# Four more gathered rows in the space of the transposed input, with an earlier first use and an earlier fetch of the residual

## The chip, the cores and the metric

The kernel runs on one core of one Trainium2 chip. The metric is the device time of one execution in microseconds; lower is better.

## The reference

The program is a decoder trunk of two layers over 256 positions of width 1024. Each layer is a mixer (latent attention in layer 0, sparse attention in layer 1) with a layer norm, and then a product-key expert network with a layer norm. The change lies in the expert network, which runs once in each layer:

```python
def peer_ffn(x, w_q, subkeys, u, v):
    ...
        q = (xc @ w_q).reshape(PEER_CHUNK, PEER_HEADS, 2, PEER_DK // 2)
        sc = jnp.einsum("thpd,hpnd->thpn", q, subkeys)
        s_half, i_half = lax.top_k(sc, PEER_TOPK)
        ...
        best, pos = lax.top_k(cand, PEER_TOPK)
        experts = jnp.take_along_axis(cand_idx, pos, axis=-1)
        g = jax.nn.softmax(best, axis=-1)
        a = jax.nn.gelu(jnp.einsum("thkd,td->thk", u[experts], xc), approximate=False)
        return jnp.einsum("thk,thkd->td", (g * a), v[experts])
...
h = layer_norm(ALPHA * h + ffn, ln_g[layer, 1], ln_b[layer, 1])
```

There are 16,384 experts (128 x 128 keys), and every token uses 128 of them: 8 heads with 16 experts each.

## The kernel before, in words

The expert network (`peer`) doesn't gather for most tokens. For the first 192 tokens (`ND`) it works densely on all experts: a table of gates is multiplied with the activations of all experts, and the second product is a plain matrix product with the whole table `p_v`. For the last 64 tokens (`GT`) the second product is made by gathering. The 128 experts of a token are laid out as 2 halves of 64, so 64 tokens fill 128 partitions, and 64 gathers of one row for each partition do it.

The stages of one layer's `peer` that matter here:

- Routing and the **u loop** (128 steps): `p_u` is streamed and multiplied with the transposed input `hT` (16 KB in each partition, written once at the layer's start and read by every u step). The activations of the last 64 tokens go to DRAM (`actD`), four steps to a DMA on GpSimd's queue (L720). Towards the end of routing, `final_gen` issues the first `RING` = 6 gathers of rows (`g_row`).
- The **v loop** (128 steps, `for j in range(P)` at L803). In each step a block of `p_v` (128 x 1024, 512 KB), loaded by SyncE through four buffers `raw`, is split by ScalarE into a rounded part `hi` (L96) and by VectorE into a rest `lo` (L107); the activations of the step are split likewise into `W` (L731 and L736). TensorE then does ten matmuls of 512 columns (`v_mm`), in the order `hi`, `lo`, `hi`, and `hi`, `lo` for the last tokens. Splits run ahead: in step j VectorE makes `lo` of block j + 2 and `W` of block j + 2.
- In the same loop the gathers are worked off. `g_act(c)`, on GpSimd's queue, gathers one activation for each partition from `actD` into column c mod 8 of the tile `gel[c // 8]` (L439). `g_mac(c)`, on VectorE, multiplies row c by its weight and adds it to `gacc` (L447 for c = 0, L449 after that). Where c is a multiple of 8 it first makes eight weights from one whole tile `gel` (L444). After each `g_mac(c)` GpSimd issues the gather of a row into the buffer that came free (`g_row`, L435), 128 rows of 4 KB.
- The residual, which was put into DRAM ahead of `peer`, is fetched back in step 100 by `reload_h` (one DMA of 1 MB on GpSimd's queue, L307), into one of the two large buffers `r8`, and the norm's factors follow in step 123 (L205).
- After the loop come the layer norm and, in layer 0, the transposition of the result into `hT`.

The order on each engine is that of the program: the kernel is scheduled by hand, and an engine that waits holds up all that stands behind it. The schedule of the v loop is these lines:

```python
            rate, gc = (P - 8 - LEAD) / 64, 0      # P = 128, LEAD = 8
...
                hi, lo = self.nxt(j < P - 2)
                w_lo(j + 2)
                w_hi(j + 3)
...
                if j < 64:
                    g_act(j)
                while gc < 64 and j >= LEAD + int(rate * gc):
                    g_mac(gc)
                    gc += 1
```

Of the kernel before, what the change touches and what calls it, by code (L numbers as in the profile page):

```python
# [12 lines left out]
F32 = mybir.dt.float32  # L13
F32R = mybir.dt.float32r
# [9 lines left out]
P = 128  # L24
S = 256
D = 1024
KC = D // P
# [6 lines left out]
FIRST, NEXT = 44, 10  # L34
GT = 64
ND = S - GT
RING, LEAD = 6, 8
GB = 1.0


class Kern:
# [88 lines left out]
    def tick(self):  # L130
        self.now += 1
        due = [f for t, f in self.later if t <= self.now]
        self.later = [x for x in self.later if x[0] > self.now]
        for f in due:
            f()

    def prep_tail(self):
        self._shi(self.si + 2)
        self._slo(self.si + 2)
# [171 lines left out]
    def build(self):  # L311
        tc, nc, I = self.tc, self.nc, self.I
        with ExitStack() as es:
# [3 lines left out]
            pers = pool(name="pers", bufs=1)  # L317
# [26 lines left out]
            self.rmseps = const.tile([P, 1], F32, name="rmseps")  # L344
            nc.vector.memset(self.rmseps, RMS_EPS)
            hN = self.r8("hN")
            self.hTT = pers.tile([P, KC, 2, S], F32R, name="hT")
            self.hT = [self.hTT[:, :, i, :] for i in range(2)]
            nc.gpsimd.dma_start(self.ident, I["c_ident"])
            nc.gpsimd.dma_start(cst, I["c_cmask"])  # L350
            with tc.tile_pool(name="xt", bufs=1) as xt:
# [54 lines left out]
    def peer(self, l):  # L406
        tc, nc, I = self.tc, self.nc, self.I
        with ExitStack() as es:
# [14 lines left out]
            gat = pool(es, "gather")  # L423
            gidx = gat.tile([P, 2, P // 2], U32, name="gidx")
# [4 lines left out]
            grow, gtable = {}, I["p_v"].rearrange("l j i d -> (l j i) d")  # L429
            gplaces = self.actD.rearrange("i j t -> (i j t)")[:, None]  # L430

            def g_row(c):
                if c < P // 2:
                    t = grow[c] = gat.tile([P, D], F32, tag="row", name="row", bufs=RING)
                    nc.gpsimd.indirect_dma_start(out=t, out_offset=None, in_=gtable,  # L435
                                                 in_offset=bass.IndirectOffsetOnAxis(ap=gidx[:, 0, c:c + 1], axis=0))

            def g_act(c):
                nc.gpsimd.indirect_dma_start(out=gel[c // 8][:, c % 8:c % 8 + 1], out_offset=None, in_=gplaces,  # L439
                                             in_offset=bass.IndirectOffsetOnAxis(ap=gidx[:, 1, c:c + 1], axis=0))  # L440

            def g_mac(c):
                if c % 8 == 0:
                    nc.vector.tensor_tensor(gw[:, c:c + 8], gel[c // 8], ggate[:, c:c + 8], op=OP.mult)  # L444
                t = grow.pop(c)
                if c == 0:
                    nc.vector.tensor_scalar(gacc, t, gw[:, 0:1], None, op0=OP.mult)  # L447
                else:
                    nc.vector.scalar_tensor_tensor(gacc, t, gw[:, c:c + 1], gacc, op0=OP.mult, op1=OP.add)  # L449
                g_row(c + RING)  # L450
            es_r, es_1 = ExitStack(), ExitStack()
            rt = pool(es_r, "route")
            oh = lambda sh, dt, name: rt.tile(sh, dt, tag="oh", name=name, bufs=8)
# [48 lines left out]
            def final_gen(tt):  # L502
# [45 lines left out]
                if tt == 1:  # L548
                    u = slice(P - GT, P)
                    nc.vector.scalar_tensor_tensor(t2[u, 0, :], sel[u, 1, :], 128.0, sel[u, 0, :], op0=OP.mult, op1=OP.add)  # L550
                    nc.vector.scalar_tensor_tensor(t2[u, 1, :], sel[u, 0, :], 128.0, sel[u, 1, :], op0=OP.mult, op1=OP.add)
                    if l:
                        nc.vector.tensor_scalar(t2[u, 0, :], t2[u, 0, :], float(l * P * P), None, op0=OP.add)
                    nc.vector.tensor_scalar(t2[u, 1, :], t2[u, 1, :], float(GT), self.tokg[u], op0=OP.mult, op1=OP.add)
                    yield 0.6
                    for hh in range(2):
                        o, c = slice(hh * GT, hh * GT + GT), slice(hh * 64, hh * 64 + 64)
                        nc.vector.tensor_copy(gidx[o], t2[u, :, c])
                        nc.vector.tensor_copy(ggate[o], sel[u, 2, c])
                    yield 0.6  # L560
                    for c in range(RING):
                        g_row(c)
# [165 lines left out]
            def w_hi(j):  # L728
                if j < P:
                    WW[j] = late[0].tile([P, 3 * P], F32R, tag="w", name="W", bufs=10) if late else W[0][:, j % 5, :]  # L730
                    nc.scalar.copy(WW[j][:, 0:ND], slot(j))  # L731

            def w_lo(j):
                if j < P:
                    for o, c in ((2 * P, slice(0, P)), (ND, slice(P, ND))):
                        nc.vector.tensor_tensor(WW[j][:, o:o + c.stop - c.start], slot(j)[:, c],  # L736
                                                WW[j][:, c].bitcast(F32), op=OP.subtract)
# [37 lines left out]
            def v_mm(j, tt, blocks, start=False, stop=False):  # L775
                hi, lo, w = kept[j]
                xh, xl, xm = w[:, 0:P], w[:, 2 * P:3 * P], w[:, P:2 * P]
                items = ((xm, hi), (xm, lo)) if tt else ((xh, hi), (xh, lo), (xl, hi))
                for a, (xx, ww) in enumerate(items):
                    go, end = start and a == 0, stop and a == len(items) - 1  # L780
                    for f in blocks:
                        self.mm(accs[tt][f], xx, ww[:, f * 512:(f + 1) * 512], go, end)

            rate, gc = (P - 8 - LEAD) / 64, 0
            summed = []

            def g_sum():

                t = gat.tile([P, D], F32, tag="row", name="gsum", bufs=RING)
                u, z = slice(P - GT, P), hN[P - GT:P, 1, :]  # L790
                nc.scalar.copy(t[u], gacc[0:GT])
                nc.vector.scalar_tensor_tensor(z, z, ALPHA, gacc[u], op0=OP.mult, op1=OP.add)
                nc.vector.tensor_tensor(z, z, t[u], op=OP.add)
# [9 lines left out]
            for j in range(P):  # L803
                if j == P - FIRST:

                    es_1.close()
                    late.append(es.enter_context(tc.tile_pool(name="late", bufs=2 * NT - 6, reuse_waits="tile")))
                    for q in range(P - NT, P - 3):
                        self.alt[self.si + q - j] = lambda: [late[0].tile([P, D], F32R, tag="keep", name="keep") for _ in range(2)]
                hi, lo = self.nxt(j < P - 2)  # L810
                w_lo(j + 2)
                w_hi(j + 3)
                if j == P - FIRST + 16:
                    hN = self.reload_h()
                if j + 4 == P - 1:
                    gb = self.load_gb(2 * l + 1)
                kept[j] = (hi, lo, WW.pop(j))
                if j < 64:
                    g_act(j)
                while gc < 64 and j >= LEAD + int(rate * gc):  # L820
                    g_mac(gc)
                    gc += 1
                if gc == 64 and not summed:
                    summed.append(1)
                    g_sum()
                v_mm(j, 0, (0, 1), j == 0, j == P - 1)
                if j < P - NT:
                    v_mm(j, 1, (0, 1), j == 0)
                    kept.pop(j)
            self.warm(AF.Sqrt)  # L830
            early = l == 0 and "nsa" in self.parts
            self.ln_start(hN, gb, accs)
# [364 lines left out]
    def nsa(self, hN, gb):  # L1197
# [4 lines left out]
        with es:  # L1202
# [108 lines left out]
            def q_tile(i, tick=True):  # L1311
                g, hf = i // 2, i % 2
                if hf == 0:
                    qps[g] = self.ps()
                hi, lo = self.nxt(tick=tick)
                self.proj_T(qps[g][:, hf * S:(hf + 1) * S], hi, lo, xhi, xlo, KC)

                def after():
                    if hf == 1:
                        ps = qps.pop(g)  # L1320
                        raws[g] = tmp.tile([64, HG, S], F32, tag="raw4", name="qr")
                        nc.scalar.copy(qu[:, g].rearrange("p a t -> p (a t)"), ps)
                        self.rope_T(tmp, ps.rearrange("p (a t) -> p a t", a=2), rT, raws[g])
                        self.defer(4, lambda: q_split(g))
                return after
# [292 lines left out]
```

## Time and profile before

| | |
|---|---|
| median of 3 runs | 1818.57 us (1818.19 to 1822.14) |
| the profiled execution | 1838.19 us, of which the span shown is 1836.4 us |
| v loop of layer 0, first matmul | 573.05 us |
| v loop of layer 1, first matmul | 1513.5 us |
| TensorE busy, VectorE busy, ScalarE busy, GpSimd busy | 96%, 87%, 57%, 28% of the span |
| mean granted TensorE clock | 0.988 of full speed |
| DMA over the span | 416.75 MB, 227 GB/s |

All times of the trace are microseconds from the start of the span. The profiled execution is some 20 us longer than the median, so differences read in the trace are added to the median. Busy shares are averages over stages with different limits, and say little of one stage.

### The profile page before, as it was taken

How to read it: one execution, taken by the hardware profiler on the slowest of the kernel's cores; microseconds unless marked ns; L12 is line 12 of the kernel's file. 1: busy time of each engine (PE TensorE's matmuls, PEld its weight loads, DVE VectorE, ACT ScalarE, POOL GpSimd, SP SyncE). 2: the span in 40 equal slices, each digit the busy share in tenths (PEclk: the TensorE clock that was granted, in tenths of full speed). 3: DMA queues.
4: the chain of work that ended last, by engine and by line, in shares of the span. 5: the costliest groups of instructions: out<-in, count | busy, mean ns of one | idle time of the engine just before them, and what ended most of it. 6: DMA issues, size and time to landing. Idle time of an engine off the chain costs nothing.

```text
span 1836.4 us, 31824 instructions
## 1 busy us (share of the span) xinstructions
PE 1769.4 (96%) x10994; PEld 1523.2 (83%) x10994; DVE 1594.4 (87%) x3782; ACT 1044.6 (57%) x2265; POOL 507.2 (28%) x457
## 2 busy tenths in 40 slices
PE   8989999999999999999898999999999999999996
PEld 6879999888888877877786689998888888777874
DVE  6778989899998988989768779988999988888988
ACT  6645455666656555555456645556666665545554
POOL 2120002000003776541542310010000007776540
PEclk9999999999999999999998999999999999999999
DMA  7445657555546998998672265656555558989993
GB/s 254 152 151 166 198 168 258 175 180 170 179 163 218 340 354 317 354 369 282 238 219 64 92 207 179 195 184 234 179 171 176 178 179 298 327 306 365 354 363 123
DMA packets 120658, 416.75 MB, mean 227 GB/s; under 512 B 18064, under 2 KB 20144, under 8 KB 119408
## 3 DMA queue, kind: packets, MB, share of 16 engines
q1 hardware_dynamic: 91008, 322.61, 52.1%
q0 software_dynamic: 29488, 92.10, 13.8%
q8 instruction: 87, 1.43, 0.3%
q14 instruction: 75, 0.61, 0.1%
HBM read 400.49 MB, written 13.63 MB: 226 GB/s over the span
## 4 chain that ended last, share of the span: by engine, by line
PE 79%; DVE 9%; DMA 4%; issue 4%; ACT 2%; POOL 0%; another core or an unknown queue 0%; SPq 0%; DVEq 0%; ACTq 0%; POOLq 0%
PE mm L153 49%; PE acc L153 29%; DMA raw<-p_v 3%; DVE lo L107 2%; DVE gacc L449 1%; ACT hi L96 1%; DVE W L736 1%; PE mm L182 1%; DMA xT<-xT 0%; DVE hN L232 0%; DMA raw<-p_wq 0%; DVE hN L250 0%; DVE m L1490 0%; DVE bnst L228 0%; DVE keep L107 0%
## 5 line engine op out<-in xcount | busy, mean ns | idle before, releaser
L96 ACT CAST hi<-raw 128x1024 fp32r<-128x1024 f32 (+1 forms) x589 | 616.8, 1049 | 406.4 <-DMA raw<-p_v 133.7
L153 PE MATMUL mm<-hT,hi 128*128 128x256 f32 (+1 forms) x3360 | 846.7, 332 | 0.0
L107 DVE TENSOR_TENSOR lo<-raw,hi 128x1024 fp32r<-128x1024 f32 (+1 forms) x582 | 709.0, 1220 | 96.7 <-ACT hi L96 68.6
L153 PE MATMUL mm<-hT,lo 128*128 128x256 f32 x2376 | 640.2, 281 | 0.0
L153 PEld LDWEIGHTS mm<-hT,hi 128*128 128x128 f32 x3360 | 560.1, 190 | 48.7 <-issue 1.2
L153 PEld LDWEIGHTS mm<-hT,lo 128*128 128x128 f32 x2376 | 451.4, 190 | 13.4
L153 PE MATMUL acc<-hi,W 128*128 128x512 f32 x1476 | 421.7, 392 | 9.1 <-ACT W L731 4.7
L153 PEld LDWEIGHTS acc<-hi,W 128*128 128x128 f32 x1476 | 277.5, 189 | 74.1 <-issue 8.6
L153 PE MATMUL acc<-lo,W 128*128 128x512 f32 x984 | 310.0, 396 | 5.8 <-DVE lo L107 4.7
L720 POOL DMA_DIRECT2D actD<-gst x64 | 34.8, 544 | 820.9 <-ACT gst L718 820.9
L435 POOL DMA_INDIRECT row<-p_v,gidx x128 | 196.5, 1535 | 166.4 <-DVE gacc L449 115.1
L153 PEld LDWEIGHTS acc<-lo,W 128*128 128x128 f32 x984 | 182.1, 189 | 57.6 <-DVE lo L107 19.2
L439 POOL DMA_INDIRECT gel<-actD,gidx x128 | 157.8, 1233 | 42.9 <-issue 38.4
L449 DVE SCALAR_TENSOR_TENSOR gacc<-row,gw,gacc 128x1024 f32<-128x1024 f32 x126 | 161.2, 1279 | 0.5
L712 ACT ACTIVATE mm<-mm 128x24 f32<-128x24 f32 (+23 forms) x168 | 40.5, 241 | 152.9 <-DVE mm L710 152.9
L736 DVE TENSOR_TENSOR W<-A,W 128x128 fp32r<-128x128 f32 (+1 forms) x512 | 109.6, 255 | 1.8 <-ACT W L731 1.8
L731 ACT CAST W<-A 128x192 fp32r<-128x192 f32 x256 | 88.1, 346 | 0.0
L710 DVE TENSOR_TENSOR mm<-mm,half 128x256 f32<-128x256 f32 x174 | 74.3, 427 | 11.3 <-ACT half L709 11.1
L613 DVE TENSOR_TENSOR A<-A,acc 128x176 f32<-128x176 f32 (+15 forms) x268 | 59.0, 273 | 25.5 <-PE acc L153 19.1
L715 ACT ACTIVATE A<-mm 128x192 f32<-128x192 f32 (+23 forms) x244 | 68.0, 278 | 12.3 <-DVE mm L710 7.3
L153 PE MATMUL acc<-hot 128*128 128x128 bf16 x1152 | 74.4, 219 | 0.0
L153 PEld LDWEIGHTS <-hot 128*128 128x128 bf16 x1152 | 66.1, 97 | 7.5 <-issue 7.5
(281 smaller groups left out, 1752.7 us busy)
## 6 DMA issues: line engine op xcount, KB each, us to landing
raw<-p_u SPq DMA_DIRECT2D x256, 512.0 KB
raw<-p_v SPq DMA_DIRECT2D x256, 512.0 KB
raw<-p_wq SPq DMA_DIRECT2D x32, 512.0 KB
actD<-gst POOLq DMA_DIRECT2D x64, 128.0 KB
raw<-b_wo SPq DMA_DIRECT2D x12, 512.0 KB
raw<-a_wo SPq DMA_DIRECT2D x8, 512.0 KB
raw<-s_wT SPq DMA_DIRECT2D x8, 512.0 KB
w<-c_w POOLq DMA_DIRECT2D x4, 1024.0 KB
```

The lines of the kernel that those rows point to most:

```text
L96: self.nc.scalar.copy(self.his[i], self.raws[i])
L107: e.tensor_tensor(self.los[i], raw, self.his[i].bitcast(F32), op=OP.subtract)
L153: self.nc.tensor.matmul(out, a, b, start=start, stop=stop)
L435: nc.gpsimd.indirect_dma_start(out=t, out_offset=None, in_=gtable, in_offset=bass.IndirectOffsetOnAxis(ap=gidx[:, 0, c:c + 1], axis=0))
L439: nc.gpsimd.indirect_dma_start(out=gel[c // 8][:, c % 8:c % 8 + 1], out_offset=None, in_=gplaces, in_offset=bass.IndirectOffsetOnAxis(ap=g ...
L449: nc.vector.scalar_tensor_tensor(gacc, t, gw[:, c:c + 1], gacc, op0=OP.mult, op1=OP.add)
L613: nc.vector.tensor_tensor(y, y, pv[:, j0:j0 + m], op=OP.mult)
L710: nc.vector.tensor_tensor(ps[:, 0:S], ps[:, 0:S], t, op=OP.add)
L712: nc.scalar.activation(ps[:, 0:n], ps[:, 0:n], AF.Gelu)
L715: nc.scalar.activation(y[:, n:ND], ps[:, n:ND], AF.Gelu)
L731: nc.scalar.copy(WW[j][:, 0:ND], slot(j))
L736: nc.vector.tensor_tensor(WW[j][:, o:o + c.stop - c.start], slot(j)[:, c], WW[j][:, c].bitcast(F32), op=OP.subtract)
```

## The change

Once the u loop has read `hT` for the last time, its 16 KB become a tile `more` of four more row buffers (`MORE` = 4); a new `hT` is taken from the same place after the v loop. The four rows 6 to 9 are issued right ahead of the v loop, and each `g_mac(c)` then issues row c + 10 in place of row c + 6. `LEAD` falls from 8 to 4: the first `g_mac` is in step 4 in place of step 8, and the last stays in step 118. The gathers of activations run eight ahead: step 0 issues eight of them, and the steps after it one each. The residual is fetched in step 11 in place of step 100.

```diff
-RING, LEAD = 6, 8
+RING, MORE, LEAD = 6, 4, 4
...
+    def new_hT(self):
+
+        self.hTT = self.pers.tile([P, KC, 2, S], F32R, tag="hT", name="hT")
+        self.hT = [self.hTT[:, :, i, :] for i in range(2)]
...
             def g_row(c):
-                if c < P // 2:
-                    t = grow[c] = gat.tile([P, D], F32, tag="row", name="row", bufs=RING)
-                    nc.gpsimd.indirect_dma_start(out=t, out_offset=None, in_=gtable,
-                                                 in_offset=bass.IndirectOffsetOnAxis(ap=gidx[:, 0, c:c + 1], axis=0))
+                if c >= P // 2:
+                    return
+                if c % (RING + MORE) >= RING:
+                    t = more[:, c % (RING + MORE) - RING]
+                else:
+                    t = gat.tile([P, D], F32, tag="row", name="row", bufs=RING)
+                grow[c] = t
+                nc.gpsimd.indirect_dma_start(out=t, out_offset=None, in_=gtable,
+                                             in_offset=bass.IndirectOffsetOnAxis(ap=gidx[:, 0, c:c + 1], axis=0))
...
-                g_row(c + RING)
+                g_row(c + RING + MORE)
...
-            rate, gc = (P - 8 - LEAD) / 64, 0
+            more = self.pers.tile([P, MORE, D], F32, tag="hT", name="more")
+            rate, gc, ge = (P - 8 - LEAD) / 64, 0, 0
+            for c in range(RING, RING + MORE):
+                g_row(c)
...
-                if j == P - FIRST + 16:
+                if j == NEXT + 1:
                     hN = self.reload_h()
...
-                if j < 64:
-                    g_act(j)
+                while ge < min(64, j + 8):
+                    g_act(ge)
+                    ge += 1
...
+            self.new_hT()
```

## Rows read from the trace of the kernel before

**Rows 1.** Page, busy engines and costliest groups (busy us, mean ns | idle before).

```profile
PE 1769.4 (96%) x10994; PEld 1523.2 (83%) x10994; DVE 1594.4 (87%) x3782; ACT 1044.6 (57%) x2265; POOL 507.2 (28%) x457
...
L449 DVE SCALAR_TENSOR_TENSOR gacc<-row,gw,gacc 128x1024 f32<-128x1024 f32 x126 | 161.2, 1279 | 0.5
```

**Rows 2.** Windows, layer 0's v loop: us, PE busy (matmuls), clock, DMA share, GB/s.

```profile
573.05:593.05 20.00, 20.00 (x90) 1.00 0.76 247
593.05:658.00 64.95, 64.95 (x288) 1.00 0.93 334
658.00:698.00 40.00, 37.84 (x152) 0.96 0.90 323
698.00:730.00 32.00, 31.41 (x136) 1.00 0.95 345
730.00:822.00 92.00, 91.94 (x402) 1.00 0.97 355
822.00:834.00 12.00, 9.36 (x34) 0.86 0.89 344
```

**Rows 3.** Windows, layer 1's v loop, the stretches with idle TensorE.

```profile
1594.00:1638.00 44.00, 40.48 (x166) 1.00 0.89 311
1638.00:1688.00 50.00, 48.37 (x210) 1.00 0.96 341
...
1764.00:1778.00 14.00, 12.61 (x51) 1.00 0.99 386
```

**Rows 4.** Timeline, GpSimd's queue around the residual: start, us [idle before <-releaser].

```profile
813.93 0.59 POOL L307 DMA_DIRECT2D hN<-hD  x1
```

**Rows 5.** Timeline, ScalarE behind that fetch.

```profile
825.59 1.04 ACT L96 CAST hi<-raw 128x1024 fp32r<-128x1024 f32 x1 [5.54 <-DMA raw<-p_v]
```

**Rows 6.** Timeline, GpSimd's queue at layer 0's first v steps.

```profile
575.01 0.54 POOL L720 DMA_DIRECT2D actD<-gst  x1 [8.73 <-ACT gst L718]
577.73 1.05 POOL L439 DMA_INDIRECT gel<-actD,gidx  x1 [2.18 <-DMA actD<-gst]
...
588.36 1.18 POOL L439 DMA_INDIRECT gel<-actD,gidx  x1 [0.30 <-issue]
```

**Rows 7.** Timeline, TensorE and VectorE at layer 0's first v steps.

```profile
573.05 0.62 PE L153 MATMUL acc<-hi,W 128*128 128x512 f32 x2
...
582.07 0.41 DVE L736 TENSOR_TENSOR W<-A,W 128x128 fp32r<-128x128 f32 x2
...
593.19 0.17 DVE L444 TENSOR_TENSOR gw<-gel,ggate 128x8 f32<-128x8 f32 x1 [1.86 <-issue]
593.39 0.76 DVE L447 TENSOR_SCALAR gacc<-row,gw 128x1024 f32<-128x1024 f32 x1
...
594.06 1.22 DVE L107 TENSOR_TENSOR lo<-raw,hi 128x1024 fp32r<-128x1024 f32 x1
```

**Rows 8.** Timeline, VectorE in layer 1: its first weights.

```profile
1533.36 0.17 DVE L444 TENSOR_TENSOR gw<-gel,ggate 128x8 f32<-128x8 f32 x1 [1.70 <-issue]
```

**Rows 9.** The tile `gel`: who waited for it (us, times).

```profile
  DVE gw L444: 3.6, 2
```

**Rows 10.** Timeline, GpSimd's queue: rows issued back to back in the u loop.

```profile
291.89 1.98 POOL L435 DMA_INDIRECT row<-p_v,gidx  x1 [9.49 <-DVE ggate L559]
...
298.59 1.04 POOL L435 DMA_INDIRECT row<-p_v,gidx  x1 [0.30 <-issue]
```

**Rows 11.** Rows issued back to back in layer 1's v loop.

```profile
1678.91 1.03 POOL L435 DMA_INDIRECT row<-p_v,gidx  x1 [0.30 <-issue]
...
1683.05 0.95 POOL L435 DMA_INDIRECT row<-p_v,gidx  x1 [0.30 <-issue]
```

**Rows 12.** Windows of 2 us behind an idle stretch: TensorE, granted clock.

```profile
690.00:692.00 2.00, 1.34 (x4) 0.85 0.24 93
692.00:694.00 2.00, 2.00 (x6) 0.50 0.72 262
694.00:696.00 2.00, 2.00 (x8) 0.80 0.60 162
```

More of the change, by code (lines that the diff above doesn't have):

```diff
@@ L346, in build @@
             hN = self.r8("hN")
-            self.hTT = pers.tile([P, KC, 2, S], F32R, name="hT")
-            self.hT = [self.hTT[:, :, i, :] for i in range(2)]
+            self.pers = pers
+            self.new_hT()
             nc.gpsimd.dma_start(self.ident, I["c_ident"])
@@ L829, in peer @@
                     kept.pop(j)
+            self.new_hT()
             self.warm(AF.Sqrt)
```

## The prediction

> **What bounds the kernel now.** I read the page first: TensorE is busy nearly throughout [rows 1], so time is lost or won where it pauses. I then cut the v loop, the only stage that the change touches, into windows. 288 matmuls in 64.95 us [rows 2] make 0.2255 us for one, so a step of ten costs 2.26 us. What a window loses is its length less its matmuls times 0.2255. In layer 0 that is 5.7 us in the window from 658, 1.3 from 698, 1.4 from 730 and 4.3 from 822, together 12.7 [rows 2]; in layer 1 it is 6.6, 2.6 and 2.5, together 11.7 [rows 3]. In these windows the DMA share is 0.89 to 0.99, and the largest pause follows the fetch of the residual: it is issued at 813.93 [rows 4], and at 825.59 ScalarE has waited 5.54 us for a block of `p_v` [rows 5]. So outside the first steps the loop is limited now and then by late blocks of `p_v`. The window from 730 moves 355 GB/s at share 0.97, so 366 GB/s at full share, and the demand at TensorE's pace is 0.524 MB x (1 + 1/1.75) in 2.26 us, or 364 GB/s: the queues are just full.
>
> The first steps differ. The DMA share is 0.76 there [rows 2], TensorE doesn't pause, and GpSimd is the engine to watch. Its gathers of activations can't start before the last write of `actD` has landed, at 577.73, and then follow back to back; the eighth starts at 588.36 and ends at 589.54 [rows 6]. VectorE's first weights need all eight. They start at 593.19, after VectorE has stood 1.86 us [rows 7], 3.65 us after the end of the eighth gather's issue. Layer 1 shows the same with 1.70 us [rows 8], and the tile's own view confirms that VectorE waited for it twice [rows 9]. So already in step 8 the first `g_mac` comes a little too early for its activations; there TensorE has enough split blocks and doesn't notice. Later VectorE doesn't set the pace: 1.22 us of `lo` and 0.41 of `W` [rows 7], and 1.28 us of `gacc` [rows 1] in one step of 1.75, come to 2.36 us for a step, less some 0.09 for each of the 2.6 instructions, which overlap by that much (593.39 + 0.76 against 594.06 [rows 7]): 2.1 us, under the 2.26.
>
> **The change, part by part.**
>
> *First use in step 4, and four rows ahead of the activations.* Nothing paces the eight first gathers of activations but GpSimd itself, so issuing them in step 0 brings none of them forward. The four rows now stand ahead of them in the same queue. They need `hT` to be free, which it is at 573.05, when the v loop's first matmul runs [rows 7]; GpSimd comes to them at 575.55, behind the last write of `actD` [rows 6]. Four rows with the way to the next instruction cost 6.7 us in the u loop (291.89 to 298.59) [rows 10], and in layer 1's v loop 1678.91 to 1684.00 and a gap of 0.30, 5.4 us [rows 11]. Some 2.2 us of that lie in the wait for `actD`'s write, which is there anyway. So the activations are pushed back by 3.2 to 4.5 us; I take 4.0. The first weights can then start at 597.2.
>
> VectorE reaches them in step 4 now. The `W` pieces from 582.07 to 582.48 [rows 7] are those of step 4 (the fifth pair of the loop), so VectorE stands from 582.5 to 597.2, almost 15 us. Behind the waiting instruction is `lo` of block 7, which step 5 makes; TensorE can finish steps 0 to 6 and two matmuls of step 7, which it has done at 573.05 + 7 x 2.26 + 0.45 = 589.3. From the start of the weights to the end of the next `lo` the trace shows 594.06 + 1.22 - 593.19 = 2.09 us [rows 7]. TensorE goes on at 599.3: a pause of 10.0 us. SyncE is held too, since it loads a block only when a `lo` frees a buffer, and GpSimd, whose row 10 waits for the first `g_mac`.
>
> After a pause the clock is lower. Behind the one near 690 the granted clock was 0.85, 0.50 (the 1.2 GHz level) and 0.80 in three windows [rows 12], which lost 0.30 + 1.00 + 0.40 = 1.7 us. I add it in full: 11.7 us for one layer, 23.4 for both. The low end is a push of 3.2 us and no lower clock, as in layer 1, whose paused windows ran at 1.00 [rows 3]: 9.2. At the high end the push is 4.5 us, the clock costs 1.7, and the four rows' 2.1 MB are still under way: the share of 0.76 leaves 0.24 x 20 us x 366 GB/s = 1.8 MB free in the first 20 us [rows 2], so 0.9 us more: 13.1.
>
> The 3.65 us from the end of the issue to the use carry a part of this. The Trainium skill (DMA: Bandwidth & Descriptors, section "Anatomy of one DMA — SWDGE (gpsimd) path") puts the fixed cost of a DMA from GpSimd's queue at some 2.0 us. By that figure the weights could start 1.65 us earlier in each layer and the change below would be 3.3 us smaller. The trace has a duration for this very gather, so I go by the trace.
>
> *Ten rows in place of six.* VectorE hardly waits for rows (0.5 us ahead of all 126 [rows 1]), so a deeper ring saves no wait directly. What moves is traffic: the same 58 rows are spread at one in 1.8125 steps in place of 1.75, a demand of 360 GB/s in place of 364. Over the 52 steps with gathers of activations that is 0.5 MB, or 1.5 us of DMA for one layer; over the 44 after them 1.3 us, of which I count half, since only 1.4 us was lost there [rows 2].
>
> *The residual in step 11.* It takes the buffer of the u loop's first ten results, which the split of block 9 frees in step 7, so it waits for nothing new. GpSimd spends 0.59 us on it [rows 4], ahead of row 14, which has 18 steps to come. The queues spend 1.05 MB / 366 GB/s = 2.9 us. What it gives back are the pauses of 4.3 and 2.5 us at its old place [rows 2, 3]. At the new place all `raw` buffers have filled during the pause just before, and the 1.5 us saved on rows cover half of its 2.9, so I count nothing there.
>
> *The rest* costs nothing: the new `hT` after the loop waits for `g_mac`s done in step 118, and the last `g_mac` stays where it was.
>
> **Sum.** Two waits, 23.4; less the residual's pauses, 6.8; less the slower rows, 2 x 0.6: +15.4 us. The profiled execution took 1838.19 us and would take 1853.6; it stands 19.6 us above the median of the runs, which profiling adds, so the difference goes on the median: 1818.57 + 15.4 = 1834.0 us. A measurement of this kernel can tell about 0.2%, 3.6 us.
>
> The savings' bounds are nothing (the late blocks only move to step 11) and all 24.4 us of later pauses. So the sum lies between 18.4 - 24.4 = -6.0 and 26.2 - 0 = +26.2: 1812.6 to 1844.8.
>
> **Rivals.**
>
> *Nothing is given back.* The residual's 2.9 us fall into a stretch with activations, rows and `p_v`, where layer 1 lost most [rows 3], and TensorE, having only just caught up with VectorE, has no `lo` in reserve. Against it: the full `raw` buffers. Then +23.4: 1842.
>
> *The relief pays for the wait.* With the gathers begun in the idle first steps, nearly all later pauses go, some 22 us of the 24.4: about 1820, no change. For it: the demand falls just under the 366 GB/s that the queues give. Against it: 1% less demand can't by itself fill pauses that had 0.89 to 0.99 of the DMA in use, and during the long wait `p_v` can run only four buffers ahead, so that time on the queues is mostly lost.
>
> *The relief is larger than the wait: faster.* Its place is the whole loop after step 8, its mechanism the free DMA time: all later pauses go (24.4) while the wait is at its low end (18.4): -6.0, 1812.6. It decides as soon as the pauses saved exceed the two waits by 3.6 us.
>
> *There is no wait*, so that the change does what its numbers suggest. The activations would have to be there by 587.2 to leave TensorE untouched; they came at 593.2 with nothing ahead of them [rows 7]. Then only the 8.0 us of savings are left: 1810.6.
>
> **How the numbers follow.** My forecast has 0.57, nothing given back 0.20, no change 0.09, the larger relief 0.11, no wait 0.03. So slower has 0.77, same 0.09, faster 0.14. The range goes from the low bound of the sum to just above the high one, 1812 to 1846, which leaves out less than 2 in 10; the forecast's own cases lie in 1826 to 1840.
>
> **What would show it.** In the changed profile VectorE's first weights (the line of L444) stand near 597 in layer 0, with an idle time of 13 to 16 us before them, and TensorE's gap ends some 2 us later, at 9 to 11 us length, in both layers, with a granted clock near 0.5 for some 3 us. On GpSimd four rows stand between the last `actD` write and the first `gel`. No pause follows the place of step 100. I'm wrong if the first weights wait less than 8 us, if the windows after step 12 lose less than 4 us in a layer, or if a new pause of more than 3 us follows the residual in step 11.

## The result, and the profile after

The changed kernel took 1833.40 us in the median of 5 runs (1828.96 to 1836.44), the kernel before 1821.60 (1818.19 to 1824.12). The ratio is 1.006, with a 95% interval of 1.004 to 1.008: slower by 7 to 15 us, some 11 us. The experiments repeat it on another occasion with 1.0042 (1.0021 to 1.0064). The ratios here and below leave out one execution of the kernel before that took 4780 us, far above all others, and stand up to 0.002 from the ratio of the two medians.

The first place to look is GpSimd's queue at layer 0's first v steps, the counterpart of [rows 6] (timeline: start, us, engine, line, operation, idle time before and its releaser; `more` are the four rows):

```profile
575.23 0.54 POOL L730 DMA_DIRECT2D actD<-gst  x1 [8.74 <-ACT gst L728]
576.07 1.25 POOL L445 DMA_INDIRECT more<-p_v,gidx  x1 [0.30 <-PE acc L158]
...
580.52 1.17 POOL L445 DMA_INDIRECT more<-p_v,gidx  x1 [0.30 <-issue]
581.99 1.18 POOL L449 DMA_INDIRECT gel<-actD,gidx  x1 [0.30 <-issue]
...
590.98 0.94 POOL L449 DMA_INDIRECT gel<-actD,gidx  x1 [0.30 <-issue]
```

The four rows stand ahead of the activations, whose first gather moved from 577.73 [rows 6] to 581.99. The eighth is issued at 590.98 to 591.92. VectorE in the same stretch, the counterpart of [rows 7]:

```profile
582.26 0.42 DVE L746 TENSOR_TENSOR W<-A,W 128x128 fp32r<-128x128 f32 x2
593.66 0.17 DVE L454 TENSOR_TENSOR gw<-gel,ggate 128x8 f32<-128x8 f32 x1 [10.98 <-DMA gel<-actD,gidx]
593.86 0.75 DVE L457 TENSOR_SCALAR gacc<-row,gw 128x1024 f32<-128x1024 f32 x1
594.53 1.22 DVE L107 TENSOR_TENSOR lo<-raw,hi 128x1024 fp32r<-128x1024 f32 x1
```

Where it stood 1.86 us before, it now stands 10.98, and the profile names the gathered activations. TensorE stops two matmuls into step 7, as VectorE has not made that block's `lo`, and goes on 6.04 us later:

```profile
589.15 0.61 PE L158 MATMUL acc<-hi,W 128*128 128x512 f32 x2
595.80 1.22 PE L158 MATMUL acc<-lo,W 128*128 128x512 f32 x2 [6.04 <-DVE lo L107]
```

Layer 1 shows the same two waits, one of VectorE and one of TensorE:

```profile
1531.80 0.17 DVE L454 TENSOR_TENSOR gw<-gel,ggate 128x8 f32<-128x8 f32 x1 [11.10 <-DMA gel<-actD,gidx]
1533.94 1.22 PE L158 MATMUL acc<-lo,W 128*128 128x512 f32 x2 [6.45 <-DVE lo L107]
```

In windows of 2 us (TensorE busy and its matmuls, granted clock, DMA share, GB/s) one sees both the clock behind that pause and what the DMA queues do in it:

```profile
588.00:590.00 2.00, 1.76 (x8) 1.00 1.04 398
590.00:592.00 2.00, 0.00 (x0) 1.00 0.21 51
592.00:594.00 2.00, 0.00 (x0) 0.91 0.02 0
594.00:596.00 2.00, 0.20 (x1) 0.50 0.03 5
596.00:598.00 2.00, 2.00 (x5) 0.50 0.62 170
598.00:600.00 2.00, 2.00 (x6) 0.50 0.47 130
600.00:602.00 2.00, 2.00 (x10) 0.88 1.02 397
```

TensorE stands from 589.8 to 595.8. The granted clock is at its lower level, 0.50 or 1.2 GHz, for the first 4 us after that pause, about as behind the pause of [rows 12]. The queues are full up to 590 and then all but empty for 5 us.

The loss of the first 30 us and of the 250 us after them, by layer, in the changed kernel:

```profile
573.30:603.30 30.00, 23.96 (x96) 0.89 0.67 240
603.30:853.30 250.00, 249.22 (x1092) 1.00 0.96 349
...
1511.00:1541.00 30.00, 23.55 (x93) 0.89 0.67 233
1541.00:1791.00 250.00, 249.11 (x1090) 1.00 0.96 349
```

At 0.2255 us for a matmul, the 30 us lose 8.4 and 9.0 us, 17.4 together; without a pause they hold 134 matmuls. The later 250 us lose 3.8 and 4.2. The prediction had named less than 4 us in a layer as a sign of being wrong, and layer 0 shows it by a hair: part of the later pauses went, though not for the reason predicted, as the section on the prediction says.

The residual is now fetched at 612.40. The longest wait of ScalarE for `p_v` behind it is 2.90 us, ending at 621.58, and TensorE doesn't pause. Its old place is nearly quiet, with 0.9 us lost in the second window against 4.3 in [rows 2]:

```profile
806.00:822.00 16.00, 16.00 (x71) 1.00 1.00 376
822.00:834.00 12.00, 11.44 (x49) 1.00 0.83 291
```

### The profile page after: what moved, and what is told of

It is laid out like the page before. It is cut to its first block, busy times and chain, and to the rows that moved or that the text cites. A ratio compares the mean times of both kernels' runs of the same rounds, so it can differ in the third digit from the quotient of the medians.

```text
span 1832.4 us, 31803 instructions
## 1 busy us (share of the span) xinstructions
PE 1764.5 (96%) x10994; PEld 1529.2 (83%) x10994; DVE 1590.6 (87%) x3782; ACT 1046.4 (57%) x2265; POOL 481.1 (26%) x457
## 4 chain that ended last, share of the span: by engine, by line
issue 39%; PE 35%; POOL 11%; DVE 7%; DMA 7%; ACT 2%; POOLq 0%; DVEq 0%; SPq 0%; ACTq 0%
PE mm L158 23%; PE acc L158 11%; POOL row L445 4%; DMA raw<-p_v 3%; POOL gel L449 3%; POOL more L445 3%; DVE lo L107 1%; POOL actD L730 1%; DMA row<-p_v,gidx 1%; DMA more<-p_v,gidx 1%; PE mm L187 1%; DMA gel<-actD,gidx 1%; ACT hi L96 1%; DVE gacc L459 1%; DVE W L746 1%
## 5 line engine op out<-in xcount | busy, mean ns | idle before, releaser
L158 PEld LDWEIGHTS acc<-lo,W 128*128 128x128 f32 x984 | 184.7, 190 | 60.8 <-DVE lo L107 23.4
L449 POOL DMA_INDIRECT gel<-actD,gidx x128 | 142.7, 1115 | 39.3 <-issue 37.5
L445 POOL DMA_INDIRECT row<-p_v,gidx x80 | 117.8, 1473 | 106.6 <-DVE gacc L459 74.1
L459 DVE SCALAR_TENSOR_TENSOR gacc<-row,gw,gacc 128x1024 f32<-128x1024 f32 x78 | 99.7, 1278 | 0.2
L445 POOL DMA_INDIRECT more<-p_v,gidx x48 | 66.9, 1394 | 46.8 <-DVE gacc L459 37.0
```

The source lines that it names most:

```text
L158: self.nc.tensor.matmul(out, a, b, start=start, stop=stop)
```

## The experiments

Single times of the kernel before spread from 1812 to 1835 us over these runs (but for the one named above), so each kernel below was timed several times beside it, and a ratio is uncertain by some 0.2%. "Early" is what the first 30 us of the two v loops lost together, by windows as above; "later" is what the 250 us after them lost; "loops" is the sum of the two loops' lengths in the profile, from the first matmul to the last. The last three columns are those of one execution each.

| kernel | ratio to before (95%) | early, us | later, us | loops, us |
|---|---|---|---|---|
| before, the profile predicted from | | 0 | 31.0 | 621.6 |
| before, profiled again | 0.9991 (0.9962 to 1.0020) | 0 | 18.6 | 608.0 |
| the change | 1.006 (1.004 to 1.008) | 17.4 | 8.0 | 615.1 |
| the change again | 1.0042 (1.0021 to 1.0064) | 17.8 | 9.3 | 617.5 |
| activations ahead of the rows | 1.0012 (0.9989 to 1.0035) | 5.6 | 14.5 | 607.0 |
| first use in step 8 | 1.0003 (0.9980 to 1.0026) | 0 | 17.7 | 606.0 |
| before, residual in step 11 | 0.9981 (0.9962 to 1.0001) | 0 | 14.3 | 599.1 |
| before, first use in step 4 | 1.0011 (0.9990 to 1.0033) | 5.7 | 16.8 | 612.1 |
| the change, residual in step 100 | 1.0048 (1.0027 to 1.0068) | 16.7 | 5.7 | 610.3 |
| the change, first use in step 2 | 1.0076 (1.0049 to 1.0103) | 25.1 | 6.4 | 617.0 |
| the change, weight by weight | 1.0038 (1.0023 to 1.0054) | 10.2 | 8.9 | 607.1 |
| both: weight by weight, activations first | 0.9989 (0.9972 to 1.0006) | 0 | 14.3 | 599.9 |
| activations first, first use in step 8 | 1.0016 (1.0001 to 1.0032) | 0 | 16.1 | 603.9 |

**The kernel before, profiled again** (no edit).

> The kernel before, unchanged, profiled once more. My theory: the change adds one wait of VectorE for activations in each layer, which costs TensorE 8 to 9 us there (17 together), and gives back only some 6, because a usual execution of the kernel before loses far less to late blocks than the 24 us in the profile that I predicted from. Then this profile shows 5 to 14 us of pauses in the two v loops and a time near 1821. Rival: 24 us of pauses are usual, profiling alone adds the 20 us, and the change costs something that I haven't found elsewhere; then this profile is at 1836 to 1840 with 20 us of pauses or more.

This profiled execution took 1827.2 us, neither the 1821 nor the 1836 that were expected, and its later windows lose 18.6 us, between the two theories as well. These are the 250 us after each loop's first 30:

```profile
605.10:855.10 250.00, 247.09 (x1077) 1.00 0.96 353
...
1536.70:1786.70 250.00, 245.65 (x1058) 1.00 0.95 351
```

They lose 7.1 and 11.4 us. The same stretches of the profile that I predicted from lose 15.0 and 15.9:

```profile
603.00:853.00 250.00, 244.46 (x1042) 0.99 0.95 345
...
1543.50:1793.50 250.00, 242.91 (x1038) 1.00 0.94 343
```

So pauses for late blocks vary from one execution to the next by as much as this change is worth, and the profile I had read was of a long execution. Nor does profiling add 20 us: in the twelve later profiles the profiled execution lies 2.4 us below to 5.0 us above the median of its kernel.

**Activations ahead of the rows.**

```diff
+            while ge < 8:
+                g_act(ge)
+                ge += 1
             for c in range(RING, RING + MORE):
                 g_row(c)
```

> The changed kernel with the first eight gathers of activations put ahead of the four rows, nothing else. My theory (the wait for the eighth activation is the loss): the rows no longer push the activations back, the first weights start some 4 us earlier (589 to 590 in layer 0), TensorE's pause shrinks from 6.4 us to about 2 and its clock falls less, so 8 to 12 us less than the changed kernel: 1821 to 1826. Rival (traffic of rows and residual early in the loop is the loss): the same traffic, so 1830 to 1836 as before.

```profile
589.43 0.17 DVE L454 TENSOR_TENSOR gw<-gel,ggate 128x8 f32<-128x8 f32 x1 [6.85 <-DMA gel<-actD,gidx]
```

The weights start at 589.43, TensorE's pause in layer 0 shrinks from 6.04 to 1.93 us, and the windows' clock stays at 1.00:

```profile
573.20:603.20 30.00, 27.96 (x121) 1.00 0.74 257
...
1507.90:1537.90 30.00, 27.61 (x120) 1.00 0.73 254
```

2.7 and 2.9 us are lost where 8.4 and 9.0 were. The ratio is 1.0012 where the change has 1.0042 to 1.006, so 5 to 9 us less; by the medians, whose ratio is 1.0032 here, it is 4 to 6. Expected were 8 to 12, and the median of 1827.87 lies 2 us above the expected times. The early loss falls by 12 us, the time by about half of that. The order of twelve gathers in one queue holds much of the early loss.

**First use in step 8.**

```diff
-RING, MORE, LEAD = 6, 4, 4
+RING, MORE, LEAD = 6, 4, 8
```

> The changed kernel with the first g_mac back in step 8 (LEAD 8, one row in 1.75 steps), the four rows, the early activations and the early residual kept. My theory: VectorE reaches the first weights near 591.5, waits some 2 us, TensorE has split blocks and doesn't pause, so the whole loss goes and the early residual and rows give a little: 1812 to 1820. Rival (traffic): rows and residual still come early, 1828 to 1836.

No early loss, 1.0003 (median 1824.30, above the expected times, but so was the kernel before with 1822.12). The early rows and the early residual carry no loss that can be seen here, so the rival falls; nor do they carry a gain. VectorE comes to the weights later than expected, at 595.81 in layer 0, and waits 0.54 us: ahead of them it has waited three times for `hi`, 5.7 us together, and ScalarE in turn 3.98 us for a block of `p_v`. TensorE has enough split blocks and doesn't notice.

**The residual alone, in the kernel before.**

```diff
-                if j == P - FIRST + 16:
+                if j == NEXT + 1:
                     hN = self.reload_h()
```

> The kernel before with the residual fetched in step 11 and nothing else. My theory: it gives back what the fetch in step 100 costs in a usual execution, 2 to 7 us of 1820: 1813 to 1819. Rival (the early fetch is a cost): 1824 to 1830.

0.9981 with an interval that just reaches 1: 0 to 7 us, so at most a small gain, and no cost; the rival falls. The median of 1821.19 lies above the expected times, and only 1 us below that of the kernel before.

**First use in step 4, in the kernel before** (six rows, residual in step 100).

```diff
-RING, LEAD = 6, 8
+RING, LEAD = 6, 4
-                if j < 64:
-                    g_act(j)
+                while ge < min(64, j + 8):
+                    g_act(ge)
+                    ge += 1
```

> The kernel before with the first g_mac in step 4 and eight activations ahead, but six rows only and the residual in step 100. My theory: the wait for the eighth activation alone is a loss; with no rows ahead of them the weights start near 589.4 as in the run with the activations first, TensorE pauses 2 to 3 us in each layer, and no early traffic gives anything back: 1.001 to 1.005 of the kernel before, with 10 to 16 us of later pauses in the profile. Rival (only the traffic of the four rows costs): no pause in the first 30 us, ratio 0.998 to 1.001.

The early loss is 5.7 us and the weights start at 589.99, as in the run with the activations first: without rows ahead of it the same wait comes, a third as dear. That pause refutes the rival; the ratio of 1.0011 is inside what was expected, but can't be told from 1 by itself. The later windows lose 16.8 us, just above the 10 to 16 expected.

**The change, with the residual back in step 100.**

```diff
-                if j == NEXT + 1:
+                if j == P - FIRST + 16:
```

> The changed kernel with the residual fetched in step 100 again. My theory: the early fetch is a gain of 2 to 5 us in the changed kernel too, so this one is slower than it: 1.007 to 1.010 of the kernel before, the same 8 to 9 us lost in the first 30 us of each layer, and 2 to 5 us more of later pauses near step 100. Rival (the early fetch is part of the loss): 1.000 to 1.005.

A miss: 1.0048, as the change itself (1.0042 beside it). Near step 100 TensorE pauses for 1.4 us in layer 1 and not at all in layer 0, less than the 2 to 5 us expected. The ratio lies in the rival's range, but the rival needs this kernel to be faster than the change, and it isn't; the early loss of 16.7 us has stayed. In the changed kernel the residual's place is worth nothing that this can measure.

**The change again** (no edit).

> The changed kernel once more, on the same chip as its variants. My theory: 1.004 to 1.008 of the kernel before, 16 to 19 us lost in the first 30 us of the two v loops together, and 4 to 8 us of later pauses. Rival (the first result was chance, since single times of the kernel before spread over 1814 to 1835): 0.998 to 1.002.

The loss is real: 1.0042, with 17.8 us of early loss. The later windows lose 9.3 us, where 4 to 8 were expected.

**First use in step 2.**

```diff
-RING, MORE, LEAD = 6, 4, 4
+RING, MORE, LEAD = 6, 4, 2
```

> The changed kernel with the first g_mac in step 2 (LEAD 2). My theory: VectorE stands from step 2, TensorE from step 5, two steps or 4.5 us sooner, while the activations come when they came; so each layer loses 4 to 5 us more at its start (13 altogether), and the ratio rises by 0.004 to 0.006 over the changed kernel's: 1.009 to 1.013. Rival (the wait is repaid by later pauses that go): the ratio stays at the changed kernel's within 0.002.

```profile
573.70:603.70 30.00, 19.92 (x79) 0.83 0.63 225
...
1517.50:1547.50 30.00, 19.97 (x76) 0.77 0.62 227
```

The early loss rises by 7 to 8 us to 25.1, as 4 to 5 us for a layer said at its lower end, but the ratio only to 1.0076: 0.0034 more than the change beside it, between the two theories. 7 to 8 us are 0.004 of the time, so this step alone doesn't tell whether a part of the longer wait comes back; each of the two ratios is uncertain by some 0.002.

**Weight by weight.** The first eight weights are made one by one, so that the first `g_mac` needs one activation.

```diff
-                if c % 8 == 0:
+                if c < 8:
+                    nc.vector.tensor_tensor(gw[:, c:c + 1], gel[0][:, c:c + 1], ggate[:, c:c + 1], op=OP.mult)
+                elif c % 8 == 0:
```

> The changed kernel with the first eight weights made one by one, each right ahead of its own g_mac, so that the first one waits for one activation in place of eight; traffic, rows, residual and rates stay as changed. My theory: the first activation lands near 585, VectorE waits 2 to 3 us, TensorE doesn't pause, nothing is lost in the first 30 us and later pauses come back to the 8 to 13 us of the kernel before: 0.997 to 1.001 of it. Rival (rows, rates and residual carry a loss of their own): 1.003 or more.

Here my theory of the wait was incomplete. The first activation's gather was issued at 582.78, and still VectorE stood until 591.64:

```profile
591.64 0.16 DVE L454 TENSOR_TENSOR gw<-gel,ggate 128x1 f32<-128x1 f32 x1 [8.16 <-DMA gel<-actD,gidx]
```

The DMA view of that one gather (count, median us from issue to landing) gives 8.8 us:

```profile
gel<-actD,gidx POOLq DMA_INDIRECT x1, 8.8
```

And the windows around it (GpSimd busy, clock, DMA share, GB/s) show the queues full until the rows are in:

```profile
576.00:582.00 6.00, 4.77 (x5) 1.00 0.70 214
582.00:590.00 8.00, 6.17 (x7) 1.00 1.00 398
590.00:592.00 2.00, 1.39 (x3) 1.00 0.64 200
592.00:594.00 2.00, 1.70 (x2) 1.00 0.03 1
```

So the rows can delay the activations in two ways: in GpSimd's queue by their issue, and on the DMA queues by their 2.1 MB. In the change itself the first is what counts, since its eighth gather is issued at 590.98, when the rows are in. The early loss of 10.2 us and the ratio of 1.0038 go with the wait that is left. The ratio lies in the rival's range, and the next run decides against the rival.

**Weight by weight, with the activations first** (both edits).

> The same with the eight gathers of activations ahead of the four rows as well. My theory: no wait at all, but what the order saved was only the wait, so the same as the run before within 0.002: 0.996 to 1.001. Rival (the rows' place matters by itself): apart from it by 0.003 or more.

With no rows ahead of it the first activation lands in 4.2 us, and VectorE goes from the split straight to the weights, without an idle time:

```profile
584.56 0.42 DVE L748 TENSOR_TENSOR W<-A,W 128x128 fp32r<-128x128 f32 x2
584.90 0.15 DVE L454 TENSOR_TENSOR gw<-gel,ggate 128x1 f32<-128x1 f32 x1
585.09 0.89 DVE L459 TENSOR_SCALAR gacc<-row,gw 128x1024 f32<-128x1024 f32 x1
```

No early loss, 0.9989. It differs from the run before by 0.005, more than the 0.002 expected and as the rival said: the rows' place matters, but through the wait, which weight by weight alone had not removed. With both edits, everything else of the change stays in and costs nothing.

**Activations first, first use in step 8** (two of the edits above).

> The changed kernel with the activations ahead of the rows and the first g_mac in step 8: all of the change's traffic, no early use. My theory: nothing lost in the first 30 us, like the run with LEAD 8 alone, 0.997 to 1.001, and so no gain that can be measured from ten rows and the early residual. Rival (the deeper ring is worth something once the wait is gone): 0.995 or less.

No early loss, 1.0016, slightly above what was expected. The deeper ring is worth nothing measurable once the wait is gone, and the rival falls; the interval leaves room for a cost of up to 6 us.

No variant beats the kernel before by more than the measurement can tell; the run with both edits is 0.5 to 0.7% faster than the change.

## Why the prediction was right, and where its terms were off

*The wait.* The mechanism came as predicted: VectorE stands in step 4, TensorE stops in step 7 after two matmuls, in both layers, and the clock drops. It is shown to be the loss: three kernels keep all of the change's transfers and lose the early pause, two of them by a later first use alone or with the activations first, one with the first use in step 4, and they stand at 0.9989, 1.0003 and 1.0016 where the change has 1.0042 to 1.006. Its dose (0, 5.6, 10.2, 17, 25 us of early loss) orders the ratios in the main; those at 0 and at 5.6 us can't be told apart.

*Its size was too large.* The term was 23.4 us for both layers and measured 17.4: pauses of 6.04 and 6.45 us where 10.0 was forecast, after waits of 10.98 and 11.10 us where 13 to 16 were. The push of 4.0 us held (581.99 against 577.73 is 4.3). What failed was the step that carried the 11.8 us of issue and the 3.65 us from the end of the issue to the use over from the kernel before. The eight gathers took 9.9 us to issue, and the last was used 1.74 us after its issue ended. The issues are shorter while VectorE stands, 0.94 or 0.95 us for each of the last seven against 0.94 to 1.79 in the kernel before; why was not tested. The windows show what goes with the quick landing: while VectorE stands, no `raw` buffer comes free, SyncE waits 11.5 us, and the queues run empty. The DMA view of the eighth gather in the changed kernel, and then of the same gather in the kernel before profiled again:

```profile
gel<-actD,gidx POOLq DMA_INDIRECT x1, 2.4
```

```profile
gel<-actD,gidx POOLq DMA_INDIRECT x1, 5.5
```

2.4 us from issue to landing on empty queues, 5.5 with `p_v` on them. The Trainium skill's fixed cost of some 2.0 us (DMA: Bandwidth & Descriptors, "Anatomy of one DMA — SWDGE (gpsimd) path"), which I set aside for the trace, comes near the first of these and not the second. The row that I preferred was taken under a load that the change itself removes at this moment. The clock's part was 4 us at 0.50, so about 2 us where I had 1.7.

*The relief.* I took 8.0 us back. Against the kernel before profiled again, the 250 us windows lose 8.0 us in place of 18.6, so 10.6 came back in this pair, and 17.4 - 10.6 = 6.8 us stands beside the measured 7 to 15. But the reason I gave, 6.8 of it for the residual, fell: its place changes nothing in the changed kernel and 0 to 7 us in the kernel before. What the runs show in its place is that the wait partly repays itself. From no early loss to 25.1 us the time rises by 14 us (9 to 19), about half. The later windows show where it comes back: they lose 14 to 19 us in the profiles without an early loss (31 in the one I predicted from), 14 to 17 after 5.6 us, 9 after 10.2, 6 to 9 after 17 and 6 after 25. With the residual back in step 100 they lose 5.7, so it isn't the residual's place. Full `raw` buffers and gathers that run ahead after the wait would do this; which of them does was not isolated.

*The base.* I predicted from a profile whose later windows lost some 12 us more than in the next one (31 against 18.6). It entered the residual's 6.8 us and the range's low end. The bound of 24.4 us for all later pauses was itself too small against these 31: short windows count the matmuls at an edge on both sides (1047 in six windows that fill layer 1's 250 us, 1038 in the whole), and two of the six, which lose some 2 us, were left out. And the queues were not full at 366 GB/s: [rows 3] already has 386 at a share of 0.99.

*The sum.* 23.4 - 8.0 = 15.4 was forecast and about 11 measured, 8 on the second occasion. The time of 1834.0 lies beside 1833.40 since the kernel before was also 3 us slower in the later runs. That hit is luck: the wait was 6 us too large, the relief was about right in size for a reason that fell, and the base was 3 us too low.

*The rivals.* That there is no wait, and that the relief is larger than the wait, fall with the idle time of 10.98 us and the ratio. That nothing is given back falls with 17.4 us of early loss against 7 to 15 us of time, and with the later windows. That the relief pays for all of it fell short by half.

## What to carry to other kernels

Before a first use is brought forward, find the last operand to arrive, and don't put a prefetch ahead of it in the same queue: both the issue and the bytes of what stands ahead can count. The deeper buffer itself brought nothing here, even with the wait gone. Where an engine works in program order, an early consumer is as dear as a late producer, since all that stands behind it waits too. And where the pauses of a stage vary between executions, profile the kernel before twice before taking a gain from them.

## What the runs showed of the hardware that was not expected

A gather of 128 activations took 2.4 us from issue to landing on empty queues, 4.2 to 5.5 us beside the stream of `p_v`, and 8.5 to 8.8 us with 2.1 MB of rows under way as well. A block of `p_v` loaded at that time, from another queue, took 8.8 and 9.3 us, and 4.1 where no rows were under way yet. So nothing here shows that the gather waits for the rows of its own queue in particular. Here the stall of VectorE emptied the queues and so shortened the wait that it was part of. For 8 us the queues moved 398 GB/s at full share, above the 366 that I had worked out from a longer window.
